# Decay rows by transposes, substitution and rotary adds on VectorE alone, and a head's tail woven into the first rotary pair

## The chip, the cores and the metric

The kernel runs on one core of one Trainium2 chip. The metric is the device time of one execution in microseconds (us). A core has five engines that take their instructions from queues in order and wait for one another by semaphores: TensorE (PE: matmuls, and PEld for its weight loads), VectorE (DVE), ScalarE (ACT), GpSimd (POOL) and SyncE (SP), which here issues nearly all of the DMAs.

## The reference

Two layers of a mixer run over 1024 prompt tokens and 32 sample tokens (1056 columns, in three token groups of 384, 384 and 288). A layer normalises its input, multiplies it by one wide weight matrix and feeds two branches:

```python
u_a, z_a, b_a, a_a, q_b, k_b, v_b, z_b, g_a, g_b = split_cols(h @ p['w_in'])
u_a, conv_new = causal_conv_silu(u_a, conv_buf, p['conv_w'])     # q, k, v of branch A, 8 heads of 128
G = jnp.cumsum(gc, axis=-1)                                       # log decay, per chunk
a_mat = jnp.eye(L) + bc[..., :, None] * kk * dec_strict           # unit lower triangular
sol = lax.linalg.triangular_solve(a_mat, rhs, left_side=True, lower=True, unit_diagonal=True)
...                                                               # scan over the chunks
q_b = rope(q_b...); k_b = rope(k_b...)                            # [x1 cos - x2 sin, x1 sin + x2 cos]
o_b = diff_attn(q_b, k_b, v_b, lam)
merged = sigmoid(g_a) * (o_a @ w_proj_a) + sigmoid(g_b) * (o_b @ w_proj_b)
x = x + gate * (merged @ p['w_out'])
```

Branch A is the gated delta rule, with a triangular system to solve in each chunk; branch B is differential attention with rotary positions.

## The kernel before

All is fp32 in effect: a weight is split into a high part (`whi`, a cast by ACT) and a low part (`wlo`, a subtraction by DVE or POOL), and each product is three matmuls. A scheduler lays out every engine's queue before the run from its own estimate of durations, taking ready instructions by priority, which is the order in which they are traced. `s.urgent()` raises what is traced inside it by `AHEAD` = 150 places. Inside `tc.manual_schedule(engines={PE})` PE keeps the order of the code.

A layer runs through these stages.

*Heads (`gdn1`, lines 544 to 641).* For each of 8 heads `conv_head` computes q, k and v: three weight tiles, each with three token groups of 24 matmuls (`pd`), which ACT copies to `u`; then the convolution on DVE, tanh on ACT. Then the chunks of 128 tokens (nine, the last of 32) are transposed four at a time into PSUM tiles `pt` (tag "pt", three buffers in this stage) and read by ACT. After the `yield` on line 591 comes what is called the head's tail here: the Exp `eg` of the decay row, `eg` times q, the mask added to `Gb`, and for each chunk three matmuls into `pt` (named `ptk`) of `kqh` (a cast by DVE) and `kql` (a subtraction by POOL, one buffer, two chunks each), an Exp `E` of `Gb`, two products by DVE (`rec` and `U`), and stores of the records `rec` (three buffers) and of `U`.

The decay row: `G` holds a chunk's tokens on the partitions. Line 474 transposes it once a layer, stores it in DRAM (`grow`), and `decay` (lines 547 to 551) loads a head's row from there into all 128 partitions, issued from ACT's queue one head ahead.

In layer 0 the modulation matmuls (`pm`) are traced between the heads.

*Handover.* After head 7, line 1424 traces rotary pair 0, outside of the manual order; lines 1431 to 1443 then trace pairs 1 to 7 inside it.

*Rotary pairs (`rope_pair`, lines 793 to 840).* Eight pairs, queries and keys in turn. For each of three token groups PE does two accumulations of 24 matmuls (`pr`), DVE four products with cos and sin (`rt`), POOL the subtraction and the addition (`ro`); the result is stored. A key group's `ro` is transposed by PE one group later (`turn_keys`, `key_rows`, tiles `ptk` from line 76).

*Substitution (`invert`, lines 653 to 679).* The triangular blocks of 64 (128 of them on the partitions), then of 32, are inverted row by row: row j is multiplied by a column of `ub` and taken from the rows below, over j + 1 columns. Columns 0 to 25 go to DVE, those from `CUT` = 26 on to POOL. After each token group of pairs 1 to 7 four values of j are traced (`next(inv)`); the rest follows the pairs.

After this come the value projection, of which 42 us (`P_INV`) are laid ahead of the first merge of the inverses, the merge and the scan, attention, and the output projections.

Of the kernel before, what the change touches and what calls it, by code (L numbers as in the profile page):

```python
# [34 lines left out]
def csize(c):  # L35
    return 128 if c < 8 else TS


class Net:
    AHEAD = 150  # L40
    CUT = 26
    LATE, P_REST, P_START = 29, 23e3, 1e3
    P_INV, P_MERGE, P_SCAN = 42e3, 3.25e3, 260.0
    P_HEAD, P_FIRST, P_SOFT, P_KEY, P_LATE, P_END = 10e3, 8e3, 500.0, 300.0, 450.0, 1e3
# [34 lines left out]
    def setup(s, st):  # L79
        tc, nc = s.tc, s.nc  # L80
        P = lambda name, bufs=1, **kw: st.enter_context(tc.tile_pool(name=name, bufs=bufs, **kw))
        s.dp = P("scratch", space=DRAM)
        s.turned = None
        s.cpool = P("const")
        s.gp = s.cpool
        s.wp = P("w", 2)
        c = s.cpool
        s.ident = c.tile([128, 128], F32, name="ident")
        s.tri = c.tile([128, 128], F32, name="tri")
        s.maskb = c.tile([128, 128], F32, name="maskb")  # L90
        s.ones = c.tile([128, 128], F32, name="ones")
        s.mhalf = c.tile([128, 72], F32, name="mhalf")
        s.ld.dma_start(out=s.ident, in_=s.io["ident"])
        nc.vector.memset(s.ones, 1.0)
        s.onesr = c.tile([128, 2], F32R, name="onesr")
        nc.vector.tensor_copy(s.onesr, s.ones[:, 0:2])
        nc.vector.memset(s.mhalf, -0.5)
        d = s.dp
        s.x1 = d.tile([T, D], F32, name="x1")
        s.x1h = d.tile([T, 512], F32, name="x1h")  # L100
        s.grow = [d.tile([NC, H, 128], F32, name=f"grow{l}") for l in range(L)]
        s.grec = [d.tile([H, NC, 128, 6, 128], F32, name=f"grec{l}") for l in range(L)]
        s.ublk = [d.tile([128, 64, 64], F32, name=f"ublk{l}") for l in range(L)]
        s.u12 = [d.tile([H, 64, 8, 64], F32, name=f"u12{l}") for l in range(L)]
        s.xblk = [d.tile([64, 64, 64], F32, name=f"xblk{l}") for l in range(L)]
        s.pblk = [d.tile([128, 64, 64], F32, name=f"pblk{l}") for l in range(L)]
        s.ublks = [d.tile([H, 32, 32], F32, name=f"ublks{l}") for l in range(L)]
        s.pblks = [d.tile([H, 32, 32], F32, name=f"pblks{l}") for l in range(L)]
        s.qscr = [d.tile([16, 64, T], F32, name=f"qscr{l}") for l in range(L)]
        s.kscr = [d.tile([16, 64, T], F32, name=f"kscr{l}") for l in range(L)]  # L110
        s.zscr = [[d.tile([8, 128, T], F32, name=f"z{l}_{i}") for i in range(4)] for l in range(L)]
        s.oascr = [d.tile([H, 128, T], F32, name=f"oa{l}") for l in range(L)]
        s.obscr = [d.tile([H, 128, T], F32, name=f"ob{l}") for l in range(L)]
        s.rrow = [d.tile([H, NC, 128], F32, name=f"rrow{l}") for l in range(L)]
        s.mscr = [d.tile([8, 128, T], F32, name=f"m{l}") for l in range(L)]
        s.grd = [d.tile([16, 128], F32, name=f"gate{l}") for l in range(L)]
# [272 lines left out]
    def gates(s, l, pool, h):  # L389
# [80 lines left out]
        s.tt(fl(s.kde), gl, G, OP.subtract)  # L470
        s.act(fl(s.kde), fl(s.kde), AF.Exp)
        s.act(fl(s.egl), gl, AF.Exp)
        pr = s.pt.tile([128, 512], F32, tag="pt", name="ptr")
        s.tr(pr[0:72, 0:128], G)
        gr = pool.tile([72, 128], F32, name="gr")
        s.cp(gr, pr[0:72, 0:128])
        s.st.dma_start(out=s.grow[l].rearrange("c h t -> (c h) t"), in_=gr)


    def conv_load(s, l, pool, ti):  # L480
# [63 lines left out]
    def gdn1(s, l, pool, h, hd, cv, gates=None):  # L544
        nc = s.nc

        def decay(hd):

            Gb = pool.tile([128, NC, 128], F32, tag="Gb", name="Gb")
            nc.scalar.dma_start(out=Gb, in_=s.grow[l][:, hd, :].partition_broadcast(128))  # L550
            return Gb

        kq, v = s.conv_head(l, pool, h, hd, cv, gates)
        k, q = kq[:, 0], kq[:, 1]

        Gb = s.decay if hd else decay(0)
        s.decay = decay(hd + 1) if hd < H - 1 else None

        kt = pool.tile([128, NC, 128], F32, tag="kt", name="kt")
        vt = pool.tile([128, NC, 128], F32, tag="vt", name="vt")  # L560
# [29 lines left out]
        s.ts(s.qe[:, :, hd], sq[:, 0], 4.0 * EPS, EPS * 128.0, OP.add, OP.mult)  # L590
        yield

        eg = pool.tile([128, NC, 128], F32, tag="eg", name="eg")
        s.act(eg, Gb, AF.Exp)
        qd = eg[:, 0:8].rearrange("p c t -> p (c t)")
        s.tt(qd, q[:, 0:TP], qd, OP.mult)
        s.tt(eg[:, 8, 0:TS], q[:, 1027:1059], eg[:, 8, 0:TS], OP.mult)
        s.tt(Gb, Gb, s.maskb.unsqueeze(1).to_broadcast([128, NC, 128]), OP.add)
        rec = s.grec[l][hd]
        s.st.dma_start(out=rec[0:8, :, 3, :].rearrange("c p t -> p c t"), in_=k[:, 0:TP].rearrange("p (c t) -> p c t", t=128))  # L600
        s.st.dma_start(out=rec[8, :, 3, 0:TS], in_=k[:, 1027:1059])
# [3 lines left out]
        for c in range(NC):  # L605
            n = csize(c)
            ps = s.pt.tile([128, 512], F32, tag="pt", name="ptk")

            if c % 2 == 0:
                c0, m = (c * 128, min(2 * 128, TP - c * 128)) if c < 8 else (1027, TS)  # L610
                parts = [pool.tile([128, 2, 2 * 128], F32R, tag=nm, name=nm)[:, :, 0:m] for nm in ("kqh", "kql")]
                x = kq[:, :, c0:c0 + m]
                nc.vector.tensor_copy(parts[0], x)
                s.tt(parts[1], x, parts[0].bitcast(F32), OP.subtract, eng=nc.gpsimd)
            y, lo = (p[:, :, c % 2 * 128:c % 2 * 128 + n] for p in parts)
            kk = ps[:n, 0:256].rearrange("p (a t) -> p a t", a=2)[:, :, :n]
            for i, (a, b) in enumerate(((y, y), (y, lo), (lo, y))):
                s.mm(kk, a[:, 0], b, start=i == 0, stop=i == 2)
            E = pool.tile([128, 128], F32, tag="E", name="E")
            s.act(E[:n, :n], Gb[:n, c, :n], AF.Exp, bias=s.nG[:n, c, hd:hd + 1])  # L620
            o = pool.tile([128, 3, 128], F32, tag="rec", name="rec")
            if c == 8:
                nc.gpsimd.memset(o[:n, 2], 0.0)
            s.act(o[:n, 0], kt[:n, c], AF.Copy, scale=ks[:n, c:c + 1])
            s.act(o[:n, 1], vt[:n, c], AF.Copy, scale=ir[:n, c:c + 1])
            s.stt(o[:n, 2, :n], ps[:n, 128:128 + n], r[:n, c:c + 1], E[:n, :n], OP.mult, OP.mult)
            if c < 8:
                s.stt(U[:, c], ps[:, 0:128], rc[:, c:c + 1], E, OP.mult, OP.mult)
                s.st.dma_start(out=rec[c, :, 0:3, :], in_=o)
            else:  # L630
                us = pool.tile([TS, TS], F32, tag="us", name="us")
                s.stt(us, ps[:n, 0:n], rc[:n, c:c + 1], E[:n, :n], OP.mult, OP.mult)
                s.st.dma_start(out=s.ublks[l][hd], in_=us)
                s.st.dma_start(out=rec[c, 0:n, 0:3, :], in_=o[:n])
        for b in range(2):
            s.st.dma_start(
                out=s.ublk[l][b * 64 + hd * 8:b * 64 + hd * 8 + 8].rearrange("c j i -> j c i"),
# [15 lines left out]
    def invert(s, l, pool):  # L653
        nc = s.nc
        for B, nb, src, xd, pdst in ((64, 128, s.ublk[l], s.xblk[l], s.pblk[l]), (32, H, s.ublks[l], None, s.pblks[l])):
            ub, X = (pool.tile([128, 4096], F32, tag=nm, name=nm)[:nb, 0:B * B].rearrange("p (a b) -> p a b", b=B) for nm in ("ub", "X"))
            for i in range(0, B, 16):
                s.ld.dma_start(out=ub[:, i:i + 16], in_=src[:, i:i + 16])
            tmp = [pool.tile([128, n], F32, tag=f"itmp{k}", name=f"itmp{k}") for k, n in enumerate((1024, 400))]
            Xf = X.rearrange("p a b -> p (a b)")  # L660
            nc.vector.memset(Xf, 0.0)
            nc.vector.memset(Xf[:, 0:B * B:B + 1], 1.0)
            for j in range(B - 1):
                m, w = B - 1 - j, j + 1

                for c0, c1, eng, k in ((0, min(w, s.CUT), nc.vector, 0), (s.CUT, w, nc.gpsimd, 1)):
                    if B == 64 and c1 > c0 or B < 64 and k == 0:
                        c1 = c1 if B == 64 else w
                        t = tmp[k][0:nb, 0:m * (c1 - c0)].rearrange("p (a b) -> p a b", b=c1 - c0)
                        s.tt(t, ub[:, j, j + 1:B].unsqueeze(2).to_broadcast([nb, m, c1 - c0]),  # L670
                             X[:, j:j + 1, c0:c1].to_broadcast([nb, m, c1 - c0]), OP.mult, eng=eng)
                        s.tt(X[:, j + 1:B, c0:c1], X[:, j + 1:B, c0:c1], t, OP.subtract, eng=eng)
                if j % 4 == 3:
                    yield
            nc.vector.tensor_copy(ub.rearrange("p a b -> p b a"), X)
# [117 lines left out]
    def rope_pair(s, l, pool, wpools, h, c_base, pr, dst, tabs, out, step=None):  # L793
# [22 lines left out]
        for g, (t0, n) in enumerate(GROUPS):  # L816
# [10 lines left out]
                        s.tt(tmp[:, :n], ps[:, :n], tab[:, sl], OP.mult)  # L827
                    tm.append(tmp)
            with s.urgent():
                s.tt(o[0][:, :n], tm[0][:, :n], tm[3][:, :n], OP.subtract, eng=nc.gpsimd)  # L830
                s.tt(o[1][:, :n], tm[1][:, :n], tm[2][:, :n], OP.add, eng=nc.gpsimd)
                for e in range(2):
                    s.st.dma_start(out=dst[pr * 4:pr * 4 + 4, e * 32:e * 32 + 32, sl], in_=o[e][:, :n])

# [509 lines left out]
    def run(s):  # L1344
# [12 lines left out]
        with ExitStack() as root:  # L1357
# [17 lines left out]
            for l in range(L):  # L1375
# [15 lines left out]
                with ExitStack() as st:  # L1391
# [8 lines left out]
                    for hd in range(H):  # L1400
# [3 lines left out]
                        else:  # L1404
                            x = s.gdn1(l, g2, h, hd, cv)
                            next(x)
                            if hd == H - 1:
                                s.conv_out(l, g1, cv)
                            drain(x)
                        if hd == 0 and mods:  # L1410
                            s.pm = psum(sm, "pmod", 1)
                            s.mod_init(s.Multi(pool(sm, "mods2", 2), pool(sm, "mods"), ("wraw","whi","wlo")))
# [8 lines left out]
                        tabs.append(tb.tile([128, T], F32, name=nm))  # L1421
                        s.ld.dma_start(out=tabs[-1], in_=io[nm])
                    wx = pool(st, f"wx{l}")
                    drain(rope(0, [wx, s.wp], None))

                vst = ExitStack()
                v1 = pool(vst, f"v1{l}", 1)
# [1 line left out]
                v2.m["vo"] = pool(vst, f"v3{l}", 2)  # L1429
                vals = s.v_proj(l, v2, h)  # L1430
                with ExitStack() as st:
                    st.enter_context(tc.manual_schedule(engines={mybir.EngineType.PE}))
                    s.pd, s.pt = psum(st, f"pdb{l}", 4), psum(st, f"ptb{l}", 2)
                    s.rop = pool(st, f"ro{l}", 4)
                    b1 = pool(st, f"b1{l}", 1)
                    b2 = s.Multi(pool(st, f"b2{l}", 2), b1, ("ko",))
# [29 lines left out]
                s.left = 24 * T / 2.4 * 40 + 2 * (8 * 24 + 16) * 512 / 2.4  # L1466
                pdc = ExitStack()
                s.pd = psum(pdc, f"pdc{l}", 2)
                order = ExitStack()
                order.enter_context(tc.manual_schedule(engines={mybir.EngineType.PE}))  # L1470

                with ExitStack() as st:
                    s.pa, s.pb, s.pt = psum(st, f"pac{l}", 3), psum(st, f"pbc{l}", 2), psum(st, f"ptc{l}", 1)
# [113 lines left out]
```

## Time and profile before

| | |
|---|---|
| median of 3 runs (lowest, highest) | 3670.26 us (3663.71, 3679.11) |
| profiled execution, its time | 3669.76 us |
| profiled execution, span from the first to the last instruction | 3667.9 us |
| mean granted PE clock over the span | 0.964 |
| DMA | 526.66 MB, 144 GB/s |

The span is what the rows below divide. "Busy" is the time in which an engine executes; a matmul's end is modelled, and matmuls overlap. A line of the code can be that of a helper: L54 is `tt`, L63 `stt`, L66 `act`, L69 `cp`, L72 `mm`, L76 `tr`. The granted clock is TensorE's: 1.0 is 2.4 GHz, 0.5 is 1.2 GHz. A wait is put down to what came last by the profile.

### The profile page before, as it was taken

Reading aid. Unit: us, or ns where it says so; the run is one execution under the profiler, and the core shown is the slowest. Engines: PE = TensorE matmul, PEld = TensorE weight load, DVE = VectorE, ACT = ScalarE, POOL = GpSimd, SP = SyncE. Lnnn points to the kernel's source line nnn. Section 1 sums busy time; section 2 is a strip of 40 time slices with the busy share of each in tenths; the row PEclk is TensorE's granted clock in tenths of the full one; section 3 lists DMA queues with packets and bytes.
Section 4 is the critical chain, followed back from the end, with each engine's and each line's share of the span. In section 5 each row is a group of like instructions: output and inputs, shape, how many; then the busy total and the mean of one; then the engine's idle time right before and its main releaser. Section 6 shows DMA issues by size and latency. Waiting matters only on the chain. (4 is left out here: it accounts for less than half of the span.)

```text
span 3667.9 us, 58186 instructions
## 1 busy us (share of the span) xinstructions
PE 3375.9 (92%) x20880; PEld 3146.5 (86%) x20880; DVE 2171.1 (59%) x3682; ACT 1507.5 (41%) x4182; POOL 1356.1 (37%) x1131
## 2 busy tenths in 40 slices
PE   8988897889999999899999899778999999999999
PEld 6887887878988998898989889778898999889897
DVE  4776669841435566765447677886033456676554
ACT  4465551113544444543244666211255344444321
POOL 2354559711124443423012224892011443343310
PEclk9999988999999999999999999889999999999999
DMA  5454542446754444546443444425576444554644
GB/s 178 114 156 130 150 144 83 110 132 196 232 150 119 135 133 135 173 145 182 142 131 96 116 120 119 119 78 152 154 229 191 125 122 132 149 152 144 181 147 149
DMA packets 618985, 526.66 MB, mean 144 GB/s; under 512 B 107028, under 2 KB 567448, under 8 KB 618312
## 3 DMA queue, kind: packets, MB, share of 16 engines
q1 hardware_dynamic: 600008, 513.50, 47.7%
q10 hardware_dynamic: 18688, 9.44, 1.4%
q8 instruction: 165, 2.70, 0.3%
q14 instruction: 124, 1.02, 0.1%
HBM read 342.49 MB, written 180.31 MB: 143 GB/s over the span
## 5 line engine op out<-in xcount | busy, mean ns | idle before, releaser
L72 PE MATMUL pd<-h,whi 128*128 128x384 f32 (+1 forms) x2688 | 700.5, 336 | 13.9 <-ACT u L69 10.4
L72 PE MATMUL pd<-mg,whi 128*128 128x384 f32 (+1 forms) x2688 | 693.3, 335 | 13.3 <-ACT u L69 12.5
L54 POOL TENSOR_TENSOR wlo<-wraw,whi 128x512 fp32r<-128x512 f32 (+1 forms) x220 | 428.1, 1955 | 554.0 <-ACT whi L69 471.9
L72 PEld LDWEIGHTS pd<-h,whi 128*128 128x128 f32 x2688 | 474.7, 193 | 21.9 <-ACT u L69 11.1
L72 PEld LDWEIGHTS pd<-mg,whi 128*128 128x128 f32 x2688 | 471.4, 192 | 21.5 <-ACT u L69 14.0
L72 PE MATMUL pd<-h,wlo 128*128 128x384 f32 (+1 forms) x1344 | 448.6, 334 | 0.0
L72 PE MATMUL pd<-mg,wlo 128*128 128x384 f32 (+1 forms) x1344 | 448.2, 333 | 0.0
L69 ACT CAST whi<-wraw 128x1024 fp32r<-128x1024 f32 (+1 forms) x304 | 258.2, 865 | 206.7 <-PE pd L72 60.3
L72 PEld LDWEIGHTS pd<-h,wlo 128*128 128x128 f32 x1344 | 258.5, 192 | 2.2 <-issue 1.2
L72 PEld LDWEIGHTS pd<-mg,wlo 128*128 128x128 f32 x1344 | 257.7, 192 | 2.9 <-issue 1.4
L72 PE MATMUL ptok<-whi,mg 128*128 128x512 f32 x768 | 240.3, 394 | 1.7 <-DVE y L54 0.8
L66 ACT ACTIVATE e<-psc,nm 32x160 f32<-32x160 f32 (+2 forms) x144 | 101.1, 702 | 330.7 <-DVE nm L1047 182.0
L54 DVE TENSOR_TENSOR wlo<-wraw,whi 128x1024 fp32r<-128x1024 f32 x84 | 107.9, 1284 | 175.8 <-ACT whi L69 174.3
L63 DVE SCALAR_TENSOR_TENSOR acc<-u,convT,acc 128x1059 f32<-128x1059 f32 x144 | 210.7, 1466 | 1.8
L72 PE MATMUL pd<-ob,whi 128*128 128x384 f32 (+1 forms) x768 | 187.2, 329 | 12.7 <-ACT ob L69 9.9
L72 PE MATMUL pr<-h,whi 128*128 128x384 f32 (+1 forms) x768 | 192.5, 337 | 1.8 <-DVE rt L54 1.8
L72 PE MATMUL pr<-mg,whi 128*128 128x384 f32 (+1 forms) x768 | 192.0, 336 | 1.9 <-DVE rt L54 1.9
L72 PE MATMUL pd<-oa,whi 128*128 128x384 f32 (+1 forms) x768 | 193.5, 331 | 0.0
L54 DVE TENSOR_TENSOR itmp<-ub,X 128x624 f32<-128x624 f32 (+56 forms) x188 | 160.2, 852 | 25.5 <-DMA ub<-ublks 16.6
L72 PEld LDWEIGHTS ptok<-whi,mg 128*128 128x128 f32 x768 | 143.4, 188 | 33.8 <-DVE y L54 1.5
L72 PE MATMUL psc<-k,qh 128*128 128x512 f32 (+3 forms) x416 | 143.1, 351 | 29.2 <-DVE e L63 29.0
L54 DVE TENSOR_TENSOR X<-X,itmp 128x624 f32<-128x624 f32 (+56 forms) x188 | 164.3, 874 | 4.9
(315 smaller groups left out, 8009.2 us busy)
## 6 DMA issues: line engine op xcount, KB each, us to landing
wraw<-in_w_in SPq DMA_DIRECT2D x160, 512.0 KB
srec<-grec SPq DMA_DIRECT2D x128, 384.0 KB
grec<-rec SPq DMA_DIRECT2D x128, 192.0 KB
z<-zo SPq DMA_DIRECT2D x96, 192.0 KB
wraw<-in_w_ada SPq DMA_DIRECT2D x64, 256.0 KB
qraw<-qscr SPq DMA_DIRECT2D x128, 128.0 KB
egt<-z SPq DMA_DIRECT2D x64, 192.0 KB
eo<-ob SPq DMA_DIRECT2D x60, 192.0 KB
```

The source lines that it names most:

```text
L54: (eng or s.nc.vector).tensor_tensor(out, a, b, op=op)
L63: s.nc.vector.scalar_tensor_tensor(out, a, sc, b, op0=op0, op1=op1)
L66: s.nc.scalar.activation(out, a, func, **kw)
L69: s.nc.scalar.copy(out, a)
L72: s.nc.tensor.matmul(out, lhsT, rhs, start=start, stop=stop)
```

## The change

The decay row is made on the chip. For each chunk a column of `nG` (minus G), repeated 128 times, is transposed into a `pt` tile; ACT takes exp of minus that into `eg`, and DVE subtracts it from the mask into `Gb`. Both are traced before the head's transposes and no longer after the `yield`; `grow` and its transfers are gone. `invert` does all columns on DVE. The rotary subtraction and addition go to DVE. Head 7's tail is cut by two more `yield`s (after chunks 2 and 5) and is traced in three parts, after the three token groups of pair 0. The manual order of PE begins ahead of pair 0 and lasts until attention is done. In the stage of pairs 1 to 7 the `pt` pool has four buffers in place of two.

```diff
@@ gates
-        pr = s.pt.tile([128, 512], F32, tag="pt", name="ptr")
-        s.tr(pr[0:72, 0:128], G)
-        gr = pool.tile([72, 128], F32, name="gr")
-        s.cp(gr, pr[0:72, 0:128])
-        s.st.dma_start(out=s.grow[l].rearrange("c h t -> (c h) t"), in_=gr)
@@ gdn1
-        def decay(hd):
-            Gb = pool.tile([128, NC, 128], F32, tag="Gb", name="Gb")
-            nc.scalar.dma_start(out=Gb, in_=s.grow[l][:, hd, :].partition_broadcast(128))
-            return Gb
         kq, v = s.conv_head(l, pool, h, hd, cv, gates)
-        Gb = s.decay if hd else decay(0)
-        s.decay = decay(hd + 1) if hd < H - 1 else None
+        Gb = pool.tile([128, NC, 128], F32, tag="Gb", name="Gb")
+        eg = pool.tile([128, NC, 128], F32, tag="eg", name="eg")
+        for c0, cn in ((0, 4), (4, 4), (8, 1)):
+            n = csize(c0)
+            pt = s.pt.tile([128, 512], F32, tag="pt", name="ptg")
+            for i in range(cn):
+                s.tr(pt[:, i * 128:i * 128 + n], s.nG[:n, c0 + i, hd:hd + 1].to_broadcast([n, 128]))
+            pv = pt.rearrange("p (c t) -> p c t", t=128)[:, 0:cn, :n]
+            s.act(eg[:, c0:c0 + cn, :n], pv, AF.Exp, scale=-1.0)
+            s.tt(Gb[:, c0:c0 + cn, :n], s.maskb[:, :n].unsqueeze(1).to_broadcast([128, cn, n]), pv, OP.subtract)
...
-        eg = pool.tile([128, NC, 128], F32, tag="eg", name="eg")
-        s.act(eg, Gb, AF.Exp)
-        s.tt(Gb, Gb, s.maskb.unsqueeze(1).to_broadcast([128, NC, 128]), OP.add)
...
+            if c % 3 == 2 and c < 8:
+                yield
@@ invert
-                for c0, c1, eng, k in ((0, min(w, s.CUT), nc.vector, 0), (s.CUT, w, nc.gpsimd, 1)):
-                    ...
+                t = tmp[0:nb, 0:m * w].rearrange("p (a b) -> p a b", b=w)
+                s.tt(t, ub[:, j, j + 1:B].unsqueeze(2).to_broadcast([nb, m, w]), X[:, j:j + 1, 0:w].to_broadcast([nb, m, w]), OP.mult)
+                s.tt(X[:, j + 1:B, 0:w], X[:, j + 1:B, 0:w], t, OP.subtract)
@@ rope_pair
-                s.tt(o[0][:, :n], tm[0][:, :n], tm[3][:, :n], OP.subtract, eng=nc.gpsimd)
-                s.tt(o[1][:, :n], tm[1][:, :n], tm[2][:, :n], OP.add, eng=nc.gpsimd)
+                s.tt(o[0][:, :n], tm[0][:, :n], tm[3][:, :n], OP.subtract)
+                s.tt(o[1][:, :n], tm[1][:, :n], tm[2][:, :n], OP.add)
@@ run
                             if hd == H - 1:
                                 s.conv_out(l, g1, cv)
-                            drain(x)
+                            else:
+                                drain(x)
...
-                    drain(rope(0, [wx, s.wp], None))
+                    order = ExitStack()
+                    order.enter_context(tc.manual_schedule(engines={mybir.EngineType.PE}))
+                    drain(rope(0, [wx, s.wp], None, lambda: next(x, None)))
+                    drain(x)
...
-                    st.enter_context(tc.manual_schedule(engines={mybir.EngineType.PE}))
-                    s.pd, s.pt = psum(st, f"pdb{l}", 4), psum(st, f"ptb{l}", 2)
+                    s.pd, s.pt = psum(st, f"pdb{l}", 4), psum(st, f"ptb{l}", 4)
...
-                order = ExitStack()
-                order.enter_context(tc.manual_schedule(engines={mybir.EngineType.PE}))
```

## Rows read from the trace of the kernel before

**Rows 1.** The page's busy time by engine, us (share of the span) x instructions.

```profile
PE 3375.9 (92%) x20880; PEld 3146.5 (86%) x20880; DVE 2171.1 (59%) x3682; ACT 1507.5 (41%) x4182; POOL 1356.1 (37%) x1131
```

**Rows 2.** Table by stretches: length, busy PE, PEld, DVE, ACT, POOL (x), clock, DMA share, GB/s.

```profile
124.00:480.00 356.00, 304.21 (x1924) 291.99 (x1923) 247.59 (x354) 214.31 (x666) 185.78 (x180) 0.93 0.52 144
541.40:769.40 228.00, 186.77 (x1075) 178.79 (x1073) 199.30 (x258) 30.94 (x62) 167.85 (x138) 0.90 0.37 105
1960.00:2260.00 300.00, 275.02 (x1747) 268.74 (x1746) 209.36 (x327) 183.71 (x596) 92.02 (x125) 0.96 0.43 117
2269.50:2313.60 44.10, 36.01 (x219) 33.91 (x218) 23.05 (x57) 27.08 (x93) 23.67 (x23) 0.89 0.43 128
2313.60:2541.40 227.80, 186.73 (x1075) 178.51 (x1073) 198.39 (x258) 31.21 (x62) 167.79 (x138) 0.90 0.37 105
```

**Rows 3.** Waits, layer 0's heads, 120 to 490 us: total, times, longest.

```profile
ACT eg L66 <- DMA Gb<-grow: 56.6, 7, 9.9
...
PE pm L72 <- ACT m L69: 22.8, 3, 8.0
PE pm L72 <- ACT whi L69: 10.2, 2, 6.5
PE pd L72 <- ACT u L69: 8.9, 2, 5.5
```

**Rows 4.** Waits, layer 1's heads, 1970 to 2260 us.

```profile
ACT eg L66 <- DMA Gb<-grow: 45.5, 7, 9.1
ACT rec L66 <- DMA grec<-rec: 19.3, 14, 2.7
...
PE ptt L76 <- ACT vt L69: 14.3, 4, 6.4
PE pd L72 <- ACT u L69: 10.5, 4, 3.6
```

**Rows 5.** Timeline, layer 1's last head: start, duration, [idle before, releaser].

```profile
2242.18 1.17 ACT L66 ACTIVATE eg<-Gb 128x1152 f32<-128x1152 f32 x1 [5.85 <-DMA Gb<-grow]
...
2244.98 0.62 PE L72 MATMUL pd<-mg,whi 128*128 128x384 f32 x2 [2.27 <-ACT u L69]
```

**Rows 6.** Table by stretches, the 4 us after one of PE's stalls.

```profile
1982.00:1986.00 4.00, 4.00 (x16) 3.82 (x16) 3.91 (x4) 3.25 (x17) 1.96 (x2) 0.58 0.73 195
```

**Rows 7.** Waits of PE and DVE, layer 0's rotary pairs, 541.4 to 769.4 us.

```profile
PE ptk L76 <- POOL ro L54: 35.2, 12, 13.0
...
DVE itmp L54 <- DMA ub<-ublks: 8.3, 1, 8.3
...
DVE X L661 <- DMA xblk<-X: 4.5, 1, 4.5
```

**Rows 8.** PE's timeline, transposes of head 7 in layer 1.

```profile
2285.77 0.93 PE L76 MATMUL ptt<-ident,kq 128*128 128x128 f32 x7
```

**Rows 9.** Timeline of layer 1's handover, and from the chain a run of `pr`.

```profile
2271.18 1.29 POOL L54 TENSOR_TENSOR wlo<-wraw,whi 128x512 fp32r<-128x512 f32 x1 [0.74 <-ACT whi L69]
...
2295.45 0.27 PE L76 MATMUL ptt<-ident,kq 128*32 128x128 f32 x1
...
2304.24 0.58 PE L72 MATMUL ptk<-kql,kqh 128*128 128x256 f32 x1 [2.51 <-POOL kql L54]
...
2487.48 18.90 PE pr L72 x120
```

**Rows 10.** Substitution in layer 0: busy DVE and POOL in its stretch, and single instructions.

```profile
541.40:729.40 188.00, 138.43 (x126) 77.62 (x74) 0.91 0.36 101
...
625.32 1.17 DVE L54 TENSOR_TENSOR X<-X,itmp 128x988 f32<-128x988 f32 x1
...
724.70 0.19 DVE L54 TENSOR_TENSOR itmp<-ub,X 128x26 f32<-128x26 f32 x1
...
635.12 0.78 POOL L54 TENSOR_TENSOR itmp<-ub,X 128x352 f32<-128x352 f32 x1
...
709.99 0.95 POOL L54 TENSOR_TENSOR ro<-rt,rt 128x288 f32<-128x288 f32 x1 [1.80 <-issue]
```

More of the change, by code (lines that the diff above doesn't have):

```diff
@@ L40 @@
     AHEAD = 150
-    CUT = 26
     LATE, P_REST, P_START = 29, 23e3, 1e3
@@ L100, in setup @@
         s.x1h = d.tile([T, 512], F32, name="x1h")
-        s.grow = [d.tile([NC, H, 128], F32, name=f"grow{l}") for l in range(L)]
         s.grec = [d.tile([H, NC, 128, 6, 128], F32, name=f"grec{l}") for l in range(L)]
@@ L658, in invert @@
                 s.ld.dma_start(out=ub[:, i:i + 16], in_=src[:, i:i + 16])
-            tmp = [pool.tile([128, n], F32, tag=f"itmp{k}", name=f"itmp{k}") for k, n in enumerate((1024, 400))]
+            tmp = pool.tile([128, 1024], F32, tag="itmp", name="itmp")
             Xf = X.rearrange("p a b -> p (a b)")
@@ L664, in invert @@
                 m, w = B - 1 - j, j + 1
-                for c0, c1, eng, k in ((0, min(w, s.CUT), nc.vector, 0), (s.CUT, w, nc.gpsimd, 1)):
[L667 to L672, printed above, removed]
+                t = tmp[0:nb, 0:m * w].rearrange("p (a b) -> p a b", b=w)
+                s.tt(t, ub[:, j, j + 1:B].unsqueeze(2).to_broadcast([nb, m, w]), X[:, j:j + 1, 0:w].to_broadcast([nb, m, w]), OP.mult)
+                s.tt(X[:, j + 1:B, 0:w], X[:, j + 1:B, 0:w], t, OP.subtract)
                 if j % 4 == 3:
```

## The prediction

> **What bounds the kernel now.** I read the busy shares first [rows 1]: TensorE (PE) is busy 92% of the span, VectorE (DVE) 59%, so time is to be won only where PE stands or is clocked low. Then the table by stretches [rows 2]; the reader is to see three kinds of place. In the delta-net heads PE is busy 304 of 356 us (layer 0) and 275 of 300 (layer 1), with granted clocks of 0.93 and 0.96. At the handover to the rotary pairs it is busy 36 of 44.1. In the rotary pairs, with the substitution beside them, it is busy 187 of 228 at 0.90, while DVE is busy 199 and POOL 168.
>
> Then the waits. In the heads ScalarE (ACT) stands once a head for the broadcast row `Gb`, 56.6 us in layer 0 and 45.5 in layer 1, and PE stands behind ACT for what ACT does late: 22.8 + 10.2 + 8.9 = 41.9 and 14.3 + 10.5 = 24.8 us [rows 3, 4]. One head shows the order: the Exp on `Gb` starts after 5.85 us of waiting, and PE's next group after 2.27 us of waiting for the copy that was queued behind it [rows 5]. After such a stall the granted clock is 0.58 over 4 us, so mostly the lower level, 1.2 GHz, and some 1.7 us of work are lost [rows 6]. In the rotary stage PE waits for POOL's rotary adds, 35.2 us in 12 waits, before the key transposes; DVE waits 8.3 and 4.5 us for the DMAs around the second substitution [rows 7].
>
> **Decay rows.** Gone: two transposes and the store of `grow`, 16 broadcast loads of 576 KB from ACT's queue, one Exp and one add of 1152 columns a head. Added a head: 9 transposes with a repeated column as the weights, three Exps and three subtractions that read PSUM, of the same columns. All of their inputs are ready since the gates, so ACT's wait for a DMA has nothing left to wait for. At stake: 41.9 + 24.8 us of standing, and 14 stalls times 1.7 us of slow clock, 24 us; together 91. What is late next: ACT's `rec` waits for the record store, 19.3 us in layer 1 in short pieces [rows 4], and PE's own order; I count three quarters as won, 68 (bounds 35 and 91). Price: seven transposes took 0.93 us, 0.13 each, and a lone one 0.27 [rows 8, 9]; none with a repeated column is in the trace, so 144 cost 19 to 39 us, and below nothing is excluded, as PE does run them. I take 0.15 each, 22 us, all on PE since it is the bound here: by the row of the run of seven, with a little for changing over. The extra fixed time of two more ACT and two more DVE instructions a head lies beside PE (DVE 209 and ACT 184 of 300 us) and costs nothing unless they move PSUM's three `pt` buffers later, which the new tiles share. Net -46 us.
>
> **Handover to the rotary pairs.** Before, from the last convolution matmul of head 7 to the memset of `X` takes 44.1 us [rows 2], alike in both layers. Pair 0's matmuls fill the 26 us (2269.5 to 2295.5) in which head 7 goes through convolution, SiLU and transposes; its 27 chunk matmuls then run bare, with stalls of 2.5 us for `kql` [rows 9]. Pair 1's first weights were split by 2272.5 [rows 9], and yet none of its matmuls went into those stalls: I read this as program order on PE holding behind all that was traced before it. Now this order begins ahead of pair 0. So pair 0 can't fill the 26 us; what it covers instead is the bare tail. New sum: 26 of latency + 144 matmuls at 18.9/120 us, 22.7, + 27 chunk matmuls at the 0.13 of the transposes, 3.5, + three waits for `kql` (single buffer, read by two chunks at a time), 7.5, makes 60; less 3, since six of pair 0's products (0.55 each, by the price below) no longer sit in DVE's queue in the latency: 57. That is +13 us a layer, +26. The head's 9 record stores and its stores of `U` go to SP's queue as before, now between the pair's own; `rec` keeps three buffers, so ACT's waits for them [rows 4] may fall between the pair's groups, where PE has matmuls to go on with. If the old order of PE persists, the tail is hidden and 10 us a layer are won; the bounds are -20 and +30.
>
> **Substitution on DVE alone.** 126 instructions a layer do the 64-blocks. 988 columns took 1.17 us and 26 took 0.19 with POOL out of the way, so one takes 0.163 us + 1.02 ns a column [rows 10]. Cut at 26 DVE has 69,082 columns (both operations, summed over j), 90.9 us by that; it was busy 138.4 [rows 10]. So 47.5 us were lost beside POOL, whose own work in that stretch is 18,278 columns at 0.78 us for 352, 40.5; 32 adds at about 1.0, 32 [rows 10]; 24 weight splits at 1.29, 31 [rows 9]: 103.5 in all. DVE loses 0.46 us for each. Full width has 87,360 columns: 109.5 us, +18.6. POOL keeps the splits alone: 31 x 0.46 = 14 lost (bounds 0 and 31), -33.
>
> **Rotary adds on DVE.** 42 a layer beside the substitution, at 0.163 us + 1.02 ns a column: 0.55 and 0.46, 22 us. POOL's queue no longer stands before the key transposes, but DVE's does: these operations are raised by 150 places, so a substitution step that falls further behind than that goes first.
>
> DVE over the 228 us stretch: 199.3 - 33 + 18.6 + 22 = 207 busy. About 13 us of the 32-block steps may slip past the last pair under the value projection: 194. Idle: 28.7 now; the waits of 8.3 and 4.5 remain, and I leave 8 more. 215 us, against 228: -13 a layer, -26. Bounds: PE alone needs 7 pairs of 22.7 and 72 transposes at 0.15, 170 us, -58; with 31 lost and nothing slipping it is 245, +17. The bigger `pt` pool helps only what waited for ACT.
>
> Sum: -46 + 26 - 26 = -46. Made against the profiled execution, 3669.8 us (span 3667.9 and 1.9 around it), 0.5 below the median: 3624.
>
> Two rules weighed against this. The Trainium skill, SBUF — State Buffer, "Who interferes with whom", has the second of two such operations block until the first is done: POOL's whole length is lost. By that DVE would lose 31 us a layer to the splits and not 14, and the sum would be 3658, between A and E below. The rows show 47.5 lost for 103.5, under half, so the trace agrees only in part. The Trainium skill, Perfetto Trace Analysis, "Optimizing Scalar/DVE Operations", says that giving work of a full DVE even to GpSimd may make sense: this change does the reverse, with DVE busy 199 of 228 us. That is the last rival below.
>
> **Rivals.**
> B, PE alone bounds the pairs: the scheduler keeps products and adds ahead of any substitution, which ends under the value projection. For it: 42 us of projection (`P_INV`) stand there as cover. Against: the raise of 150 places, about two token groups. 45 us more a layer: 3534.
> C, old order at the handover, and all 91 us won: 3624 - 23 - 46 = 3555. Against: what [rows 9] show of pair 1.
> D, other waits take the place of the `Gb` ones, as PE's order was planned around them: half won, 45 - 22, so -23; handover +26; pairs -6: 3667.
> E, slower: DVE is the bound of the pairs and its loss doesn't shrink. Place: the substitution's middle, steps of up to 1.2 us with key transposes behind adds that are behind them. If the loss stays at 47.5, 33 us a layer come back: 3690. It decides from where the loss stays above some 37 us a layer, since 23 of the 33 eat the 46 won. For it: DVE's share; against: two thirds of POOL's work is gone.
>
> **How the numbers follow.** A (the sum) 0.41, own range 3590 to 3652; B 0.10; C 0.15; D 0.20; E 0.14. Faster or slower means beyond 0.5%, 18 us, about what can be told from no change: A, B and C are faster, 0.66; D within, 0.20; E 0.14. The range goes from just below C to E, 3545 to 3690.
>
> **What would show it.** Right: no wait of ACT's Exp for a DMA; PE's waits for ACT in the heads under 20 us in all; granted clock there above 0.96; the substitution's 126 instructions at 120 to 128 us busy; a hole on PE of some 20 us before pair 0; 64-blocks ending about 188 us after their memset, as now, but the last pair only some 25 us later. Wrong: pair 0's matmuls among head 7's transposes; most of the widest substitution instructions still at 1.6 us; PE waiting for `ro` more than 35 us a layer.

## The result, and the profile after

The changed kernel takes 3557.73 us (median of 4 runs, 3554.91 to 3559.45) against 3671.74 for the kernel before on the same chip: ratio 0.9689, 95% interval 0.9667 to 0.9711. That is 114 us less, where 46 were forecast. By the first and last instructions of each stage in the two profiled executions (us; "heads" begin at the layer's first work, the pairs at the memset of `X`, the cover with the first matmul `ptok` of the value projection, the rest with the first merge matmul `ptm`):

| stage | layer 0 | layer 1 | both | forecast |
|---|---|---|---|---|
| heads | 451.1 → 406.1 | 373.0 → 341.4 | -76.6 | -46 |
| handover | 44.0 → 52.3 | 44.1 → 62.9 | +27.1 | +26 |
| pairs | 226.1 → 179.4 | 225.8 → 180.0 | -92.5 | -26 |
| cover up to the merge | 47.1 → 58.5 | 47.2 → 59.1 | +23.3 | 0 |
| rest | 1082.0 → 1084.2 | 1078.4 → 1081.1 | +4.9 | 0 |

The page's busy time, to be read beside [rows 1]: POOL has 266 us less, DVE hardly more, and PE's share has risen because the span shrank.

```profile
PE 3356.4 (94%) x21022; PEld 3134.2 (88%) x21022; DVE 2178.3 (61%) x3810; ACT 1509.0 (42%) x4212; POOL 1089.8 (31%) x887
```

The table by stretches (columns as in [rows 2]): heads of layer 0 and handover, pairs and cover; then the same of layer 1.

```profile
124.00:440.00 316.00, 303.28 (x2021) 290.31 (x2021) 241.80 (x375) 214.49 (x691) 195.67 (x181) 0.99 0.51 148
452.40:504.80 52.40, 39.44 (x224) 36.47 (x221) 28.61 (x65) 25.42 (x89) 16.17 (x16) 0.85 0.34 99
504.80:684.10 179.30, 171.19 (x1076) 168.89 (x1076) 173.53 (x239) 32.45 (x64) 44.11 (x27) 0.99 0.44 126
684.10:742.60 58.50, 46.60 (x200) 37.99 (x199) 39.14 (x89) 7.41 (x14) 0.00 (x0) 0.91 0.46 133
1890.00:2150.00 260.00, 260.00 (x1726) 256.19 (x1725) 198.67 (x322) 174.57 (x552) 80.05 (x119) 1.00 0.38 110
2168.20:2231.20 63.00, 46.98 (x247) 41.33 (x245) 32.86 (x85) 32.99 (x119) 21.31 (x20) 0.77 0.31 92
2231.20:2411.20 180.00, 173.00 (x1076) 170.38 (x1075) 175.66 (x237) 32.02 (x63) 42.74 (x27) 0.98 0.44 125
2411.20:2470.30 59.10, 46.60 (x200) 37.99 (x199) 40.72 (x91) 8.03 (x14) 0.00 (x0) 0.90 0.46 133
```

In this stretch of layer 1's heads PE never stands (260.00 of 260 us, clock 1.00); in the pairs it stands 8 of 179 us, where it stood 41 of 228. The cover shows the reverse: 58.5 us long, PE busy 46.6. The same stretch of the kernel before (same columns) had hardly any idle time:

```profile
767.50:814.60 47.10, 46.45 (x206) 37.10 (x204) 14.21 (x32) 7.59 (x15) 3.48 (x4) 1.00 0.53 135
```

The waits of the kernel after (total, times, longest): first layer 0's heads (against [rows 3]), then its pairs (against [rows 7]), then the cover of layer 0 and of layer 1.

```profile
ACT rec L65 <- DMA grec<-rec: 20.4, 11, 2.9
...
ACT eg L65 <- PE ptg L75: 2.9, 3, 1.5
...
PE pd L71 <- ACT u L68: 1.5, 1, 1.5
...
PE ptk L75 <- DVE ro L53: 7.7, 3, 5.7
...
PE ptm L71 <- DMA mu<-u: 11.9, 1, 11.9
...
PE ptm L71 <- DMA mu<-u: 12.5, 1, 12.5
```

The 56.6 us of ACT behind `Gb` are gone, and of PE's 35.2 behind `ro` 7.7 are left; what is new is one wait a layer at the merge. The handover of layer 1 on PE's timeline (against [rows 9]): pair 0 starts directly behind head 7's last convolution matmul, among the last transposes of head 6. Head 7's own 27 transposes begin behind pair 0's first group, in the last row but one. A decay tile (`ptg`) ahead of them waits for DVE, and later chunk matmuls wait for POOL.

```profile
2168.18 0.27 PE L75 MATMUL ptt<-ident,kq 128*32 128x128 f32 x1
2168.21 0.42 PE L71 MATMUL pr<-mg,whi 128*128 128x384 f32 x1
2168.47 0.27 PE L75 MATMUL ptt<-ident,v 128*32 128x128 f32 x1
...
2191.50 1.33 PE L75 MATMUL ptg<-ident,nG 128*128 128x128 f32 x5 [3.74 <-DVE U L62]
2192.76 1.11 PE L75 MATMUL ptt<-ident,kq 128*128 128x128 f32 x4
...
2229.38 0.22 PE L71 MATMUL ptk<-kql,kqh 128*32 128x64 f32 x1 [3.47 <-POOL kql L53]
```

The substitution's 64-blocks on DVE, in both layers, and one of the widest instructions (against [rows 10]):

```profile
504.80:705.50 200.70, 121.86 (x126) 0.98 0.46 131
2231.20:2434.30 203.10, 117.91 (x126) 0.98 0.46 129
...
609.74 1.21 DVE L53 TENSOR_TENSOR X<-X,itmp 128x1024 f32<-128x1024 f32 x1
```

### The profile page after: what moved, and what is told of

The parts are those of the page before. It is cut to its first block, busy times and chain, and to the rows that moved or that the text cites. A ratio compares the mean times of both kernels' runs of the same rounds, so it can differ in the third digit from the quotient of the medians.

```text
span 3554.3 us, 58233 instructions
## 1 busy us (share of the span) xinstructions
PE 3356.4 (94%) x21022; PEld 3134.2 (88%) x21022; DVE 2178.3 (61%) x3810; ACT 1509.0 (42%) x4212; POOL 1089.8 (31%) x887
## 4 chain that ended last, share of the span: by engine, by line
PE 41%; DVE 7%; DMA 6%; ACT 2%; issue 1%; POOL 1%; SPq 0%; DVEq 0%; POOLq 0%; ACTq 0%
PE pd L71 22%; PE ptok L71 8%; PE pr L71 2%; DMA eo<-ob 2%; PE pav L71 2%; PE psc L71 2%; PE pts L71 1%; DVE X L53 1%; DVE itmp L53 1%; PE pta L75 1%; DMA srec<-grec 1%; PE po L71 1%; PE ptk L71 1%; DVE ro L53 1%; PE ptt L75 1%
## 5 line engine op out<-in xcount | busy, mean ns | idle before, releaser
L53 POOL TENSOR_TENSOR wlo<-wraw,whi 128x512 fp32r<-128x512 f32 (+1 forms) x220 | 439.0, 2004 | 844.9 <-ACT whi L68 776.3
L71 PE MATMUL pd<-oa,whi 128*128 128x384 f32 (+1 forms) x768 | 192.0, 329 | 0.0
L71 PE MATMUL pr<-h,whi 128*128 128x384 f32 (+1 forms) x768 | 184.9, 326 | 0.0
L53 DVE TENSOR_TENSOR itmp<-ub,X 128x63 f32<-128x63 f32 (+36 forms) x188 | 140.4, 747 | 19.5 <-DMA ub<-ublks 11.7
L71 PE MATMUL ptok<-wlo,mg 128*128 128x512 f32 x384 | 150.7, 395 | 0.0
## 6 DMA issues: line engine op xcount, KB each, us to landing
grec<-rec SPq DMA_DIRECT2D x128, 192.0 KB
z<-zo SPq DMA_DIRECT2D x96, 192.0 KB
egt<-z SPq DMA_DIRECT2D x64, 192.0 KB
eo<-ob SPq DMA_DIRECT2D x60, 192.0 KB
```

The lines of the kernel that those rows point to most:

```text
L53: (eng or s.nc.vector).tensor_tensor(out, a, b, op=op)
L71: s.nc.tensor.matmul(out, lhsT, rhs, start=start, stop=stop)
```

## The experiments

All times are medians; ratios are to the kernel before, run on the same chip. Differences between two changed kernels are taken from the medians, often across chips; the kernel before gave 3667.7 to 3671.7 us there, so such a difference of 4 us or less says nothing. In the expectations, the "theory" is what was thought most likely before the run, the "rival" the best other account.

**The parts alone, each put into the kernel before.** First the decay rows (the hunks of `gates` and `gdn1`, without the two added `yield`s).

> The kernel before with the decay rows made by transposes, and nothing else of the change. In the kernel after, the heads of both layers became 45.0 + 31.3 = 76.3 us shorter, against 46 forecast. Theory: this edit alone does it; all 91 us at stake come back and the 144 transposes cost only some 15 us, so the time falls by about 76, to 3595 (3585 to 3605), and the handover and the pairs keep their 44 and 226 us. Rival, my forecast's sizes: three quarters are won and the transposes cost 22, so 3626; what is missing then came from the other edits, such as POOL being free earlier.

3610.7 us, ratio 0.9841 (0.9822 to 0.9860), 58 less. The heads got 45.5 and 33.0 us shorter, as the theory had it. But the handover became 1.5 and 8.6 longer and the pairs 5, so the time lies between theory and rival. The table by stretches of this kernel's heads, layers 0 and 1, reads as the kernel after's:

```profile
124.00:440.00 316.00, 302.71 (x2018) 289.87 (x2017) 240.91 (x376) 214.63 (x690) 195.00 (x180) 0.99 0.51 148
1930.00:2200.00 270.00, 270.00 (x1802) 266.07 (x1801) 204.78 (x328) 184.58 (x596) 84.97 (x121) 1.00 0.39 113
```

Then the substitution, the additions, and both:

```diff
- for c0, c1, eng, k in ((0, min(w, s.CUT), nc.vector, 0), (s.CUT, w, nc.gpsimd, 1)): ...
+ t = tmp[0:nb, 0:m * w]...; s.tt(t, ..., OP.mult); s.tt(X[:, j + 1:B, 0:w], ..., t, OP.subtract)
```

> The kernel before with the whole substitution on VectorE; the rotary additions stay on POOL. Theory (order of the queues): the pairs were held by POOL's additions standing in POOL's queue behind substitution operations. With these gone the additions are done at once, and VectorE's products, which are raised, go ahead of the substitution: the stretch from the memset of X to the first value projection matmul falls from 226 to about 182 us a layer, the substitution ends later than now under the value projection, and PE waits some 12 us for the merge's first DMA; net about 28 us a layer, 3615. Rival (load of VectorE, as in my forecast): the pairs follow VectorE's busy time. Full width adds 18.6 us, and POOL's 63 us of additions and splits still cost VectorE 0.46 each, 29 in place of 47.5: busy time and stretch stay as they are, 226, and the time is 3671.

```diff
- s.tt(o[0][:, :n], tm[0][:, :n], tm[3][:, :n], OP.subtract, eng=nc.gpsimd)
+ s.tt(o[0][:, :n], tm[0][:, :n], tm[3][:, :n], OP.subtract)     # and o[1] alike
```

> The kernel before with the rotary additions on VectorE; the substitution stays split at column 26. Theory (order of the queues): PE's waits for POOL before the key transposes go, so the pairs fall to about 182 us a layer here as well; the substitution, with its POOL part, ends under the value projection, with some wait at the merge: 3605 to 3625. Rival (load of VectorE): VectorE gets 22 us more and loses 15 fewer beside POOL, so the stretch grows by about 7 us a layer: 3685.

> The kernel before with the substitution and the rotary additions on VectorE, with the old handover, the old decay rows and two pt buffers. Theory: the pairs take 180 us in place of 226, and about 15 us of it are given back at the merge: 31 us a layer, 3609. Rival, my forecast's size for this part: 13 us a layer, 3645; then the rest of the pairs' gain in the kernel after came from the four pt buffers or the order of PE.

Substitution alone: 3624.7 (0.9876, 0.9859 to 0.9893), pairs 201.7 and 199.2. Additions alone: 3656.7 (0.9964, 0.9951 to 0.9977), pairs 221.4 and 215.5. Both: 3617.7 (0.9863, 0.9840 to 0.9885), pairs 192.0 and 188.7, cover 54.9. Neither theory held for the single edits: each alone is worth less than the order of the queues promised, and the load of DVE would have given no gain at all. With both, 51 us are gained, near the theory's 62 and twice the 26 forecast. The pairs with both edits still are 9 to 13 us longer than in the kernel after; in layer 0 of the kernel with both, PE's waits say for what (`ko` is ACT's copy of a key tile), and the timeline shows why at one of them: the copy is queued behind a scaling that waits for a weight DMA. The first line is layer 0 of the kernel before (two expectations below say 3.0 for it), the next two the kernel with both.

```profile
PE ptk L76 <- ACT ko L69: 3.9, 9, 1.0
...
PE ptk L76 <- ACT ko L69: 19.7, 11, 9.9
PE ptk L76 <- DVE ro L54: 0.5, 1, 0.5
```

```profile
579.95 1.06 ACT L66 ACTIVATE wraw<-wraw 128x1024 f32<-128x1024 f32 x1 [10.24 <-DMA wraw<-in_w_in]
...
583.04 0.63 ACT L69 COPY ko<-ptk 128x256 f32<-128x256 f32 x2
...
583.44 0.61 PE L76 MATMUL ptk<-ident,ro 128*32 128x128 f32 x2 [9.92 <-ACT ko L69]
```

**The `pt` buffers of the pairs.**

```diff
- s.pd, s.pt = psum(st, f"pdb{l}", 4), psum(st, f"ptb{l}", 4)      # kernel after
+ s.pd, s.pt = psum(st, f"pdb{l}", 4), psum(st, f"ptb{l}", 2)
```

> The kernel after with two pt buffers in the pairs, as before, and all else kept. With substitution and additions alone on VectorE, PE waited 19.7 us a layer for ACT's copy ko of the key tiles, which it had not done before (3.0) and does not do in the kernel after. Theory: the four buffers hide that copy. With two, the pairs take about 191 us in place of 179.5, some 4 us a layer of it come back at the merge, PE's waits for ko are near 20 us: 3570 (3563 to 3578). Rival: the 10 us a layer between the two kernels come from the weave or from PE's single order, ko is hidden anyway: 3558.

3573.1 (0.9738, 0.9714 to 0.9762): 15 more than the kernel after, pairs 192.8 and 191.5, cover 54.6. PE waits for the copy again in layer 0's pairs:

```profile
PE ptk L75 <- ACT ko L68: 14.7, 12, 5.5
```

The reverse edit (two to four buffers) went into the kernel with the additions alone and into the kernel before.

> The kernel before with the rotary additions on VectorE and four pt buffers; the substitution stays split with POOL. With the additions alone PE waited 33.3 us a layer for ACT's ko and 7.0 for the additions, and the pairs took 221 and 215 us. Theory: the additions on POOL were only the later of two waits of about one size, the copy ko the other; with both gone the pairs fall to about 190 us a layer although the substitution still uses POOL, with some of it given back at the merge: 3610 (3600 to 3625). Rival: the two engines' loss beside each other in the substitution holds the pairs, they stay above 210 and the time is 3650.

> The kernel before with four pt buffers in the pairs and nothing else. With the additions on VectorE these two buffers more were worth some 20 us a layer (pairs 221 and 215 against 201 and 197). Theory: in the kernel before the copy ko ends ahead of POOL's additions at nearly every key group (waits 3.0 against 35.2), so alone they bring nothing: 3662 to 3668. Rival: they are worth the same here, 3630.

3623.0 (0.9869, 0.9850 to 0.9888) and 3663.0 (0.9984, 0.9973 to 0.9995). With the additions on DVE the two buffers bring 34 us, the pairs going from 221 to 201, not to the 190 expected: the split substitution does cost something (PE waits 17.8 us for DVE's additions there). In the kernel before they bring 7. So `ko` was a second wait, hidden under that for POOL.

**The weave.** Tail of head 7 whole ahead of pair 0, PE's order begun behind it.

```diff
                             if hd == H - 1:
                                 s.conv_out(l, g1, cv)
-                            else:
-                                drain(x)
+                            drain(x)
...
-                    order = ExitStack(); order.enter_context(...)
-                    drain(rope(0, [wx, s.wp], None, lambda: next(x, None)))
-                    drain(x)
+                    drain(rope(0, [wx, s.wp], None))
+                    order = ExitStack(); order.enter_context(...)
```

> The kernel after with head 7's tail traced whole ahead of pair 0 and PE's manual order begun behind pair 0, as before; four pt buffers, decay rows, substitution and additions as after. Theory: the weave costs; with the decay rows alone the handover took 45.5 and 52.7 us, in the kernel after 52.3 and 62.9, so the time falls by 17, to 3540, and the pairs stay at 179 us. Rival: the weave is worth the 10 us a layer by which the pairs of the kernel after beat those with the substitution and the additions alone: 3561 or more. By my forecast's size for the handover (+13 a layer) it would be 3532.

3543.9 (0.9663, 0.9639 to 0.9686), by the medians 14 less than the kernel after, by the handovers 12: 47.2 and 56.2 in place of 52.3 and 62.9. The pairs stay at 179.7. The intervals of the two ratios overlap, but the handovers are as short in the two other versions without the weave (46.8 to 46.9 and 53.8 to 56.1), and with 56 us of cover (below) the same edit is worth 16. The weave costs, and buys nothing; how much of it is the tail's place and how much PE's earlier order, changed together here, is not shown.

**The cover of the merge.** `P_INV` from 42e3 to 56e3 in the kernel after.

> The kernel after with 56 us instead of 42 us of value projection laid ahead of the first merge (P_INV). Theory: PE's wait for the merge's first DMA (11.9 and 12.5 us), in which the substitution's slip is paid, is covered and the work laid ahead is only moved: 22 to 25 us less, 3534. Rival: the 14 us are missing later in the merge and the scan, where they fill PE's latencies: the first wait goes and others of the same size come, 3550 to 3560.

3527.6 (0.9612, 0.9594 to 0.9630), 30 less, more than the 22 to 25 expected. PE's wait at the merge falls by 8.6 and 10.2 us, to 3.3 and 2.3; the other 11 were won behind it, and why is open. Layer 0 in this kernel, 11.9 in the kernel after:

```profile
PE ptm L71 <- DMA mu<-u: 3.3, 1, 3.3
```

**The transposes' price.**

```diff
+                for _ in range(2):
                     s.tr(pt[:, i * 128:i * 128 + n], s.nG[:n, c0 + i, hd:hd + 1].to_broadcast([n, 128]))
```

> The kernel after with each of the 144 transposes of the decay column made twice into the same place; only the price is doubled. Theory: eight of them start within 0.84 us in the kernel after (0.105 each), PE is busy all through the heads, so 144 more cost 15 us: the heads 7 to 8 us longer a layer, 3573. Rival, my forecast's price of 0.15: 22 us, 3580. Rival, they lie in PE's waits: 3558.

The heads got 7.6 and 6.3 us longer: 13.9 for the 126 that stand there (the other 18 are head 7's, in the handovers), 0.11 each, close to the 0.105 of the theory. Yet the whole time, 3555.1 (0.9694, 0.9672 to 0.9716), is that of the kernel after: the handovers were 1.6 and 5.5 us shorter and the stages behind the merge some 10. Why these gave it back is open.

**VectorE's order in the pairs.** DVE's queue in the order of the code, with four and with two substitution steps (values of j) behind each token group.

```diff
+ st.enter_context(tc.manual_schedule(engines={mybir.EngineType.PE, mybir.EngineType.DVE}))
  s.pd, s.pt = psum(st, f"pdb{l}", 4), psum(st, f"ptb{l}", 4)
...
- if j % 4 == 3:      # only in the second of the two
+ if j % 2 == 1:
```

> The kernel after with VectorE's queue in the pairs kept in the order of the code: four steps of the substitution behind each token group, so that 79 of the 94 steps stand ahead of the last group's products. The scheduler's own queue has 50 there in the kernel after (81 in the kernel before). Theory: the pairs became short because VectorE's queue lets the substitution slip behind them. With 29 more steps, the turning of X and its DMA waits ahead of the last groups, the pairs take some 210 us, near the 215 of my forecast, and PE's wait at the merge goes: 19 us a layer more, 3596 (3580 to 3610). Rival: PE runs ahead far enough that VectorE's order doesn't matter, and the pairs stay near 180: 3558 or, with the wait at the merge gone, 3535.

> The kernel with VectorE's queue in the order of the code, with two steps of the substitution behind each token group in place of four; 40 of the 94 steps then stand ahead of the last group's products (50 in the kernel after, 79 with four steps). Four steps gave 3658: pairs of 233 us, PE waiting 29.2 us for the additions and 26.0 for the products in layer 0. Theory: it is the number of steps ahead of the products that sets the pairs, 4 steps are up to 10 us on VectorE and 3.2 of rotary work where PE needs 8; two are up to 5 us and fit. The pairs come back to about 180 us; ten steps more than in the kernel after lie behind them, so PE's wait at the merge grows by some 5 to 10 us: 3570 to 3580. Rival: the fixed order itself holds PE back, whatever the number, since each group must wait for the products in turn: the pairs stay above 205 and the time above 3610.

Four steps: 3658.2 (0.9969, 0.9956 to 0.9982); handover and pairs together take 297 us in layer 0 where the kernel after has 232 and the kernel before 270, more than the theory's price. Two steps: 3600.5 (0.9823, 0.9806 to 0.9840); together 231, so the number of steps decides and not the fixed order. But the merge waits 33.9 us, far over the 5 to 10 expected on top of 11.9. PE's waits in the pairs with four steps, then in the pairs and the cover with two:

```profile
PE ptk L75 <- DVE ro L53: 29.2, 8, 10.0
PE pr L71 <- DVE rt L53: 26.0, 5, 11.4
```

```profile
PE ptk L75 <- DVE ro L53: 9.7, 1, 9.7
...
PE ptm L71 <- DMA mu<-u: 33.9, 1, 33.9
```

**Together.** No weave, with 56 and with 62 us of cover.

> The kernel after without the weave (tail of head 7 whole ahead of pair 0, order begun behind pair 0) and with 56 us of value projection ahead of the first merge. Alone the first gave 3543.9 and the second 3527.6, where the kernel after has 3557.7. Theory: they lie in different stages and add: 13.8 + 30.1 less, 3514 (3508 to 3520). Rival: without the weave the pairs end earlier against the substitution, or the projection's cover runs out, and a part is lost: 3520 to 3528.

> The kernel after without the weave and with 62 us of value projection ahead of the first merge; with 56 us it gave 3511.9 and PE still waited 3.5 us for the merge's first DMA in layer 0. Theory: this wait goes in both layers, 7 us less: 3505. Rival: what is laid ahead is missing later, the same wait comes back in the merge or the scan: 3510 to 3515.

3511.9 (0.9571, 0.9548 to 0.9594): the two gains add, and this is the fastest version, 46 us below the changed kernel. With 62 us 3517.7 (0.9594, 0.9573 to 0.9616): no gain beyond 56.

## Why the prediction was wrong

Faster was right, and the time lay in the range; the size was 2.5 times too small. By the steps:

**Pairs: the step that failed.** The forecast made the pairs as long as DVE's load: 194 us busy and 21 idle, 215. DVE's queue was to hold the key transposes: "these operations are raised by 150 places, so a substitution step that falls further behind than that goes first", and only "about 13 us of the 32-block steps may slip past the last pair". In the trace of before, 81 of the 94 steps (63 values of j in the 64-blocks, 31 in the 32-blocks) had begun ahead of the last group's products; after, 50, where the order of the code would have 79. At four steps a group the substitution had fallen some seven token groups behind, and the raise was taken to stop it at about two; why it slipped past the raise no run shows. In layer 0, 41 steps, 31 us of work and a part of the 64-blocks among them, begin under the value projection (12 steps and 9 us before). The substitution ends 61 us behind the last pair, 16 before; the 64-blocks, forecast to end some 25 us ahead of the last pair, end 20 behind it. DVE is still busy 173.5 of the 179.3 us, but PE waits for it for 7.7 only. How many steps stand ahead does decide: code order with 79 ahead lost 65 us a layer up to the end of the pairs, with 40 ahead none. So PE all but alone bounded the pairs (171.2 us busy): rival B's mechanism, given 0.10. B put the pairs at 170 us and the sum at 215; they took 179.4 and 180.0. B also counted the 42 us of projection as cover enough. They were too few: 11.9 and 12.5 us of waiting at the merge, which 56 us of cover took nearly away.

**A term set at nothing.** "The bigger `pt` pool helps only what waited for ACT" gave it no time in the sum. In the kernel before 7 us were to be gained; in the kernel after, where the copy `ko` was the next wait in line, 15. I did not ask what was late next behind `ro`.

**The substitution's own cost held, the additions' roughly.** 121.9 and 117.9 us for the 126 instructions, against 120 to 128; the 42 additions took 24.4 and 29.9 us, against 22. DVE lost 12.4 and 8.4 us over its own 109.5 beside POOL, where 14 were taken.

**Decay rows: mis-sized.** The mechanism came as told: ACT waits for no DMA at its Exp, and PE's waits for ACT in the heads are some 2 us. "I count three quarters as won, 68" failed: with this edit alone the heads fell by 78.5, which with the 13.9 of the transposes makes 92, all of the 91 at stake. The price was taken at 22 for all 144; at 0.11 each it is 16. Against that, the edit's own 10 us at the handover were not in the sum. The prediction named the condition, "costs nothing unless they move PSUM's three `pt` buffers later", and there it came in part: head 7's `ptg` tiles stand ahead of its other transposes, and PE waits for a `pt` buffer that DVE still reads, 3.74 us in layer 1 (the row above) and 4.72 in layer 0:

```profile
468.06 1.09 PE L75 MATMUL ptt<-ident,v 128*128 128x128 f32 x4 [4.72 <-DVE Gb L53]
```

In the kernel with the decay rows alone such waits are 2.8 us, so most of its 10 us stays open.

**Handover: the size by accident.** 27 us came where 26 were forecast, but some 12 to 14 are the weave's and 10 the decay rows'; the last 3 to 5 are open. The picture was half wrong: no hole of 20 us stood ahead of pair 0. Its first group's 48 matmuls ran in head 7's latency, beside head 6's last transposes and chunk matmuls, ahead of head 7's own, so neither the hole nor the sign named against the forecast came in the form given. Only the other two groups were held behind the chunk matmuls, with `kql` still waited for (3.47 us).

The Trainium skill, SBUF — State Buffer, "Who interferes with whom", lets a DVE instruction with two SBUF inputs contend with a GpSimd instruction that reads SBUF. In the kernel with four steps in code order three of the widest instructions stood beside two weight splits:

```profile
601.74 1.22 DVE L53 TENSOR_TENSOR itmp<-ub,X 128x1020 f32<-128x1020 f32 x1
601.74 4.60 POOL L53 TENSOR_TENSOR wlo<-wraw,whi 128x512 fp32r<-128x512 f32 x2 [2.83 <-ACT whi L68]
603.00 2.19 DVE L53 TENSOR_TENSOR X<-X,itmp 128x1020 f32<-128x1020 f32 x1
605.23 2.20 DVE L53 TENSOR_TENSOR itmp<-ub,X 128x1023 f32<-128x1023 f32 x1
```

The first of DVE's lost nothing; then both engines pay: 2.2 us against 1.21 for DVE's, 2.30 against 1.29 [rows 9] for one of POOL's. The five end after 5.7 us, where one after the other they would take 6.2: they nearly take turns. The trace agrees with the rule here. Over the whole stretch little is left of it, since few of POOL's operations remain.

The Trainium skill, Perfetto Trace Analysis, "Optimizing Scalar/DVE Operations", also warns that moving work between GpSimd and DVE may not help, as they share a port. That half of the rule fits these runs better than the half weighed in the prediction: work given back to the busier engine was worth 51 us. That the port is the reason is not shown: what went with it is PE's wait behind POOL's queue.

## What to carry to other kernels

An engine with a high busy share is no bound if its queue lets the work that nobody waits for slip: count in the trace how much of it stands ahead of each operation that the bounding engine needs. What slips must be paid where its result is first used, so the cover there has to grow with it. When a wait goes, look for the one underneath, such as a buffer freed by a third engine.

## What the runs showed of the hardware

In these pairs a stall cost more than its length. In layer 0 PE was busy 186.8 us for 1075 matmul records at a granted clock of 0.90 [rows 2] and 171.2 us for 1076 at 0.99 after: some 15 of the 46 us won are the clock's, once the long waits were gone. And a transpose with a repeated column cost PE 0.11 us in a busy stage, no more than a plain one in a run, 0.13 [rows 8].
